# PSUM pool ends, operand tiles and load placement in a two-layer feed-forward block on one Trainium2 core

## The chip, the core and the metric

One core of one Trainium2 chip runs the whole program in one launch. The metric is device time in microseconds (us). Before the change the median of three runs is 2013.85 us (2013.82 to 2015.16). The core has five engines with queues of their own: PE (TensorE, matrix products), DVE (VectorE), ACT (ScalarE), POOL (GpSimd) and SP (which here only issues transfers). PE reads both operands from the on-chip memory SBUF and writes into PSUM, which has eight banks of 2 KiB per partition.

## The reference

One encoder layer on x of 512 rows and 2048 columns, all float32. The parts that matter here come last:

```
h = RMSNorm(x); z = h @ w_in; A = MLA(z); N = neighbourhood attention(z)
x = x + concat(RMSNorm(A), RMSNorm(N)) @ w_out
x = x + relu(RMSNorm(x) @ w_ff1)^2 @ w_ff2        # d_ff = 8192
y = RMSNorm_final(x)
```

## The kernel before, in words

Every float32 operand is kept as two tiles, a rounded high part ("hi") and the remainder ("lo"), and every block product is three matmuls: hi by hi, lo by hi, hi by lo (`mm3`, L100; `prod`, L287 and L968). `split` (L90) makes the two parts: a cast on ACT (L92 or L95), a subtraction on DVE (L93 or L96).

The program runs through attention until 540 us of the profile, the output projection "wo" until about 702 us, and then the two feed-forward products.

**From the projection to the first product.** The projection is made in four column blocks n. For each, the new x is written to DRAM (`x_d`), scaled (`hs`), transposed by PE into PSUM tiles `ht` (L811), and `mix` (L750) makes from the four `ht` tiles the operands of the first product: a11, a12, a22 and the sums s1 to s4 of a Strassen scheme, each as hi and lo and in two halves g. The `ht` tiles lie in pool `ps_ax` (`sct`, `trt`, `pvt`, four banks), projection results in pool `ps_mm` (`mmt`, four banks). After the last `mix` both pools are closed and a pool `ps_w` is opened over the same eight banks, with four tiles of two banks:

```
close_pool("ps_ax")
close_pool("ps_mm")
ps_w = open_pool("ps_w", space=PSUM)
def wide(name): return ps_w.tile([P, 2, 512], F32, name=name, tag="w", bufs=4)
```

**First product** (`ff1_pair`, L858, calling `strassen_t`, L285). 32 pairs of column blocks; each pair is seven products (a11, a12, s2, s1, s3, s4, a22, in this order) of 24 matmuls with 256 columns, accumulated into PX, PY and PZ, each in the first bank of a `wide` tile. The moving operand is an a or s tile, the weights of the array are the block of w_ff1 (tiles `ob`, `ot`). Nine of the operand pairs lie in pool `ops1`, one pool tile per operand part of 2*UNIT+16 elements (UNIT is 1024; 8,256 bytes), three more in slots of pool `iop` at an offset of 8 elements, two in other pools. A finished pair is squared by ACT and written to DRAM, the part a to `f_d`, sums of it to `s_d`.

**Second product.** It takes the 8192 rows of w_ff2 in nine chunks (`CH`, L31): a plain one of 512 (`plain`, L935: eight groups of 24 matmuls with 512 columns, tiles `f`), seven of 1024 made by a Strassen scheme (`spair`, L950: two pairs per chunk, each of seven products of 24 matmuls, tiles `sx`, `sy`, `sz`; I call one such call a Strassen pair), and a plain one of 512 at the end (tiles `f2l`). Here the reloaded first result is the weights (`fo`, loaded by `load_op`, L929, into the `ops1` tiles at an offset of 8 elements) and w_ff2 is the moving operand (tiles `hi` and `lo` of pool `wp`, and by `f2_bufs`, L906, every third time an `ops1` tile). Raw loads of 512 KB go through three buffers (`raw_unit`, L70). The seven `fo` operands of the first Strassen chunk are loaded ahead of the plain chunk. DVE adds every finished PSUM tile into the sum SF.

**Tail.** x is read back from `x_d` (`load_x1`, L1033) into four operand pairs (`xf`), SF and the last chunk are added, and the final norm is written out.

The order on each queue is set by a scheduler that follows program order and the readiness of buffers.

Of the kernel before, what the change touches and what calls it, by code (L numbers as in the profile page):

```python
# [36 lines left out]
def block_kernel(ctx, tc, x, xT, w_c, w_ckv, w_qkv, w_uqn, w_uqr, w_ukv, rpb, gcols, w_out, w_ff1, w_ff2, g_fin,  # L37
# [17 lines left out]
    ps_mm = open_pool("ps_mm", space=PSUM)  # L55
    ps_ax = open_pool("ps_ax", space=PSUM)

# [226 lines left out]

    def strassen_t(nm, getA, b, m1, tile, v, t2, pst=None):  # L285

# [10 lines left out]
        b11, b21, b12, b22 = b  # L297
        PX, PY, PZ = ((pst or mmt)(f"p{x}{nm}")[:, :256] for x in "xyz")
        prod(PX, "a11", opB(f"ob11{nm}", b11), True)
# [374 lines left out]

    def wide_tile(pool, name, tag, off, bufs=1, dt=F32R):
        return pool.tile([P, UNIT + 16], dt, name=name, tag=tag, bufs=bufs)[:, off:off + UNIT]

    def op_pair(nm, g, name, off):
        t = ops1.tile([P, 2 * UNIT + 16], F32R, name=name, tag=f"{nm}_{g}")
        return [t[:, off + j * UNIT:off + (j + 1) * UNIT] for j in range(2)]  # L680

    def iot(name, off=0):
        return [wide_tile(iop, f"{name}_{j}", f"io{j}", off, 4) for j in range(2)]

# [55 lines left out]
    def opt(pool, nm, g):  # L740
        if pool is iop:
            t = iot(f"{nm}_{g}", 8)
        elif pool is ops1:
            t = op_pair(nm, g, f"{nm}_{g}", 0)
        else:
            t = [pool.tile([P, UNIT], F32R, name=f"{nm}_{g}_{j}") for j in range(2)]
        A[nm][g] = [v.rearrange("p (k n) -> p k n", k=4) for v in t]
        return A[nm][g]
# [39 lines left out]
    for n in range(4):  # L788
# [4 lines left out]
        if n == 3:  # L793
            first = [wide_tile(iop, f"b{kh}1_0", f"io{kh}", 0, 4, F32) for kh in range(2)]
            for kh in range(2):
                nc.sync.dma_start(out=first[kh], in_=w_ff1[kh, 1])
# [61 lines left out]
    def ff1_pair(i):  # L858
# [3 lines left out]
        t2 = sb(rk, "t2", i, UNIT, 1) if i else wp.tile([P, UNIT], F32, name="t2_0", tag="raw", bufs=3)  # L862
        PX = strassen_t(f"_{i}", getA, b, sb(rk, "m1", i, 256, 1), lambda t, w: sb(rk, t, i, w, 1), v, t2,
                        lambda s: wide(s)[:, 0])
        nc.scalar.activation(v[0][:, 256:], PX, AF.Relu)
# [15 lines left out]
    close_pool("ps_ax")  # L881
    close_pool("ps_mm")
    ps_w = open_pool("ps_w", space=PSUM)

    def wide(name):
        return ps_w.tile([P, 2, 512], F32, name=name, tag="w", bufs=4)

    for i in range(DFF // 256):
        ff1_pair(i)
    close_pool("rk")  # L890
    close_pool("vp")


# [6 lines left out]

    def op_tiles(nm, g, name):
        return op_pair(nm, g, name, 8)

    nb = [0]

    def f2_bufs(name):  # L906
        i = nb[0] % 6
        nb[0] += 1
        return unit_bufs(name) if i < 4 else op_tiles(("a11", "s3")[i - 4], 1, name)

# [7 lines left out]
    def load_f(c, q):  # L918
        raw = raw_unit(f_d[c][:, :, q, :], f"fa{c}_{q}", 4)
        t = blocks(op_tiles(("a11", "a12")[q], 0, f"fa{c}_{q}") if c else iot(f"fa{c}_{q}"))  # L920
        split(t[0], t[1], raw)
        F.setdefault(c, []).append(t)
# [6 lines left out]
    def load_op(c, nm):  # L929
        raw = raw_unit((f_d if nm[0] == "a" else s_d)[c][:, BLK[nm]], f"fo{c}_{nm}", 4)  # L930
        t = blocks(op_tiles(nm, 0, f"fo{c}_{nm}"))
        split(t[0], t[1], raw)
        FO[c, nm] = t
# [16 lines left out]
    def spair(c, j, k0, hook):  # L950
# [4 lines left out]
        def ld(kh, nh, u):  # L955
            name = f"sb{kh}{nh}_{nm}_{u}"
            if nh == 0:
                t = wide_tile(iop, name, f"io{kh}", 0, 4, F32)
            else:
                t = fb.tile([P, UNIT], F32, name=name, tag=("b12", "b22")[kh], bufs=2)  # L960
            nc.sync.dma_start(out=t, in_=w_ff2[k0 // 256 + kh * nu + u, 2 * j + nh])
            return t
# [68 lines left out]
    RF = 36  # L1031

    def load_x1(m):  # L1033
        xs = []
        for h, t in enumerate(op_tiles(("s3", "s4", "a22", "a11")[m], m // 3, f"xf{m}")):
            t = t.bitcast(F32)
            xs += [t[:, :512], t[:, 512:]]
        for n in range(4):
# [4 lines left out]
    for n in range(4):  # L1043
        if n == 1:
            xfs = [load_x1(0)]
        for g in range(2):
# [19 lines left out]
    for m in range(NM):  # L1066
# [18 lines left out]
        for n in (0, 3, 1, 2):  # L1085
# [77 lines left out]
```

## Time and profile before

| | |
|---|---|
| Median of three runs | 2013.85 us |
| Profiled execution | 2013.5 us, span 2011.7 us |
| PE busy | 1968.0 us (98% of the span), 12540 instructions |
| DVE busy | 1573.3 us (78%) |
| ACT busy | 1005.1 us (50%) |
| Mean granted PE clock | 0.994 of full speed |

The span is what the engines' instructions cover; 1.8 us of the execution lie around it. PE is nearly always busy, but a matmul's length is not fixed: the interval from one start to the next is what counts. The clock column of a stretch is the granted share of the full clock (2.4 GHz); 0.5 is the lower level of 1.2 GHz.

### The profile page before, as it was taken

How to read it: one execution, taken by the hardware profiler on the slowest of the kernel's cores; microseconds unless marked ns; L12 is line 12 of the kernel's file. 1: busy time of each engine (PE TensorE's matmuls, PEld its weight loads, DVE VectorE, ACT ScalarE, POOL GpSimd, SP SyncE). 2: the span in 40 equal slices, each digit the busy share in tenths (PEclk: the TensorE clock that was granted, in tenths of full speed). 3: DMA queues.
4: the chain of work that ended last, by engine and by line, in shares of the span. 5: the costliest groups of instructions: out<-in, count | busy, mean ns of one | idle time of the engine just before them, and what ended most of it. 6: DMA issues, size and time to landing. Idle time of an engine off the chain costs nothing.

```text
span 2011.7 us, 31103 instructions
## 1 busy us (share of the span) xinstructions
PE 1968.0 (98%) x12540; PEld 1775.4 (88%) x12540; DVE 1573.3 (78%) x1892; ACT 1005.1 (50%) x1435; POOL 64.0 (3%) x73
## 2 busy tenths in 40 slices
PE   8999999999999979999999999998999999999997
PEld 7999999888887779999999999997888888888886
DVE  7777777787435767787878787875799999999995
ACT  5645445566314545555555555554454454444443
POOL 2000010100000000000000000000000000000000
PEclk9999999999999989999999999999999999999999
DMA  8354454431334333545454444455364354444342
GB/s 279 131 180 154 160 167 139 143 102 58 119 107 157 120 132 122 183 138 178 140 175 143 172 146 169 153 168 214 126 196 168 117 178 160 143 158 156 126 165 97
DMA packets 121552, 303.75 MB, mean 151 GB/s; under 512 B 10688, under 2 KB 49344, under 8 KB 121152
## 3 DMA queue, kind: packets, MB, share of 16 engines
q1 hardware_dynamic: 98416, 271.09, 40.7%
q10 hardware_dynamic: 22224, 29.52, 4.1%
q8 instruction: 98, 1.61, 0.3%
q0 software_dynamic: 768, 1.15, 0.2%
q14 instruction: 46, 0.38, 0.1%
HBM read 250.60 MB, written 52.26 MB: 151 GB/s over the span
## 4 chain that ended last, share of the span: by engine, by line
PE 91%; DVE 3%; DMA 3%; ACT 1%; issue 1%; POOL 1%; SPq 0%; POOLq 0%; DVEq 0%; ACTq 0%
PE px L292 7%; PE px L293 7%; PE px L294 7%; PE sx L980 5%; PE sx L979 5%; PE sx L981 5%; PE pz L293 4%; PE pz L292 4%; PE pz L294 4%; PE wo L102 3%; PE wo L103 3%; PE wo L104 3%; PE sz L979 3%; PE sz L981 3%; PE sz L980 3%; PE py L292 2%
## 5 line engine op out<-in xcount | busy, mean ns | idle before, releaser
L190 DVE TENSOR_TENSOR SF<-SF,sx 128x1024 f32<-128x1024 f32 x56 | 68.1, 1216 | 2.3 <-PE sx L981 1.1
L190 DVE TENSOR_TENSOR sb<-sb,sb 128x1024 f32<-128x1024 f32 x56 | 67.2, 1220 | 0.5
L92 ACT CAST s_0hi<-sb 128x1024 fp32r<-128x1024 f32 x28 | 29.5, 1052 | 41.5 <-PE sx L981 18.4
L128 POOL TENSOR_TENSOR stat<-stat,nhalf 128x1 f32<-128x1 f32 (+1 forms) x6 | 4.4, 730 | 1401.5 <-DVE stat L127 1401.5
L92 ACT CAST a<-sb 128x1024 fp32r<-128x1024 f32 x30 | 31.5, 1050 | 32.1 <-PE sz L981 15.3
L92 ACT CAST a_0hi<-sb 128x1024 fp32r<-128x1024 f32 x27 | 28.4, 1052 | 35.4 <-PE sz L981 17.1
L92 ACT CAST s<-sb 128x1024 fp32r<-128x1024 f32 x28 | 29.4, 1050 | 30.8 <-PE sx L981 16.5
L93 DVE TENSOR_TENSOR a_0lo<-sb,a_0hi 128x1024 fp32r<-128x1024 f32 x27 | 33.0, 1221 | 13.3 <-ACT a_0hi L92 13.3
L93 DVE TENSOR_TENSOR a<-sb,a 128x1024 fp32r<-128x1024 f32 x30 | 36.6, 1220 | 7.5 <-ACT a L92 7.5
L868 ACT ACTIVATE v<-v 128x512 f32<-128x512 f32 x64 | 40.5, 632 | 2.0
L867 ACT ACTIVATE v<-v 128x512 f32<-128x512 f32 x64 | 40.3, 630 | 1.4 <-DVE v L190 0.3
L92 ACT CAST a_1hi<-sb 128x1024 fp32r<-128x1024 f32 x27 | 28.3, 1047 | 23.8 <-PE sz L981 17.1
L92 ACT CAST s_1hi<-sb 128x1024 fp32r<-128x1024 f32 x28 | 29.4, 1049 | 19.2 <-PE sx L981 18.8
L190 DVE TENSOR_TENSOR b<-b,b 128x1024 f32<-128x1024 f32 x32 | 38.9, 1215 | 0.0
L93 DVE TENSOR_TENSOR s_0lo<-sb,s_0hi 128x1024 fp32r<-128x1024 f32 x28 | 34.2, 1221 | 4.5 <-ACT s_0hi L92 4.5
L93 DVE TENSOR_TENSOR s<-sb,s 128x1024 fp32r<-128x1024 f32 x28 | 33.8, 1220 | 2.6 <-ACT s L92 2.6
L190 DVE TENSOR_TENSOR SF<-SF,sz 128x1024 f32<-128x1024 f32 x28 | 34.1, 1216 | 1.8 <-PE sz L981 1.7
L190 DVE TENSOR_TENSOR sb<-st,sb 128x1024 f32<-128x1024 f32 x28 | 34.1, 1219 | 0.1
L190 DVE TENSOR_TENSOR st<-sb,sb 128x1024 f32<-128x1024 f32 x28 | 34.1, 1219 | 0.1
L93 DVE TENSOR_TENSOR s_1lo<-sb,s_1hi 128x1024 fp32r<-128x1024 f32 x28 | 34.1, 1218 | 0.0
L93 DVE TENSOR_TENSOR a_1lo<-sb,a_1hi 128x1024 fp32r<-128x1024 f32 x27 | 32.9, 1218 | 0.0
L93 DVE TENSOR_TENSOR wo_2lo<-wo_2r,wo_2hi 128x1024 fp32r<-128x1024 f32 x8 | 9.8, 1224 | 27.9 <-ACT wo_2hi L92 27.9
(2897 smaller groups left out, 8300.5 us busy)
## 6 DMA issues: line engine op xcount, KB each, us to landing
sb<-in_w_ff_dram SPq DMA_DIRECT2D x112, 512.0 KB, 4.5
b<-in_w_ff_dram SPq DMA_DIRECT2D x64, 512.0 KB, 5.9
f_d<-v ACTq DMA_DIRECT2D x32, 512.0 KB, 6.7
s_d<-sv SPq DMA_DIRECT2D x28, 512.0 KB, 6.4
nb<-in_w_qkv_dram SPq DMA_DIRECT2D x24, 512.0 KB, 4.5
xn<-in_x_dram SPq DMA_DIRECT2D x8, 512.0 KB, 4.9
X<-in_x_dram SPq DMA_DIRECT2D x16, 256.0 KB, 5.4
wo_0r<-in_w_out_dram SPq DMA_DIRECT2D x8, 512.0 KB, 4.4
```

The costliest lines, as they stand in the source:

```text
L92: i = nc.scalar.copy(hi, src)
L93: nc.vector.tensor_tensor(out=lo, in0=src, in1=hi.bitcast(F32), op=ALU.subtract)
L102: nc.tensor.matmul(ps, ah, bh, start=first, stop=False)
L103: nc.tensor.matmul(ps, ah, bl, start=False, stop=False)
L104: nc.tensor.matmul(ps, al, bh, start=False, stop=last)
L190: nc.vector.tensor_tensor(out=out, in0=a, in1=b, op=op)
L292: nc.tensor.matmul(ps, bh, ah, start=first and kk == 0, stop=False, **kw)
L293: nc.tensor.matmul(ps, bh, al, start=False, stop=False, **kw)
L294: nc.tensor.matmul(ps, bl, ah, start=False, stop=kk == 7, **kw)
L979: nc.tensor.matmul(ps[:, mm], ah, bh, start=first and kk == 0, stop=False, **kw)
L980: nc.tensor.matmul(ps[:, mm], ah, bl, start=False, stop=False, **kw)
L981: nc.tensor.matmul(ps[:, mm], al, bh, start=False, stop=kk == 2 * nu - 1, **kw)
```

## The change

**PSUM.** `ps_ax` opens at the other end of PSUM; `ps_mm` keeps the first four banks, `ps_ax` the last four. PX, PY and PZ of the first product are now `mmt` tiles of `ps_mm`, which stays open until the first product is over. The wide tiles of the second product come from two pools of two tiles, one over the banks of `ps_ax`, one over those of `ps_mm`.

**Operands.** The `ops1` tiles become two tiles, `op_a` of six operand pairs and 64 more elements, and `op_b` of three pairs and 48 more. Operand parts follow each other at 1024 elements; the first product uses them at offset 0, the second at offset 8. Slots of `iop` lose their 16 extra elements and their offset.

**Loads.** The seven `fo` loads of the first Strassen chunk are placed two after each block n of the plain chunk; the two loads of the last chunk's `fa` follow products a11 and a12 of the last Strassen pair. x is read back for three row blocks into a tile `xb` that takes the place of all of `op_b`, and for the fourth into a tile of its own.

```diff
-    ps_ax = open_pool("ps_ax", space=PSUM)
+    ps_ax = open_pool("ps_ax", space=PSUM, side="right")
...
-        PX, PY, PZ = ((pst or mmt)(f"p{x}{nm}")[:, :256] for x in "xyz")
+        PX, PY, PZ = (mmt(f"p{x}{nm}")[:, :256] for x in "xyz")
...
-    def wide_tile(pool, name, tag, off, bufs=1, dt=F32R):
-        return pool.tile([P, UNIT + 16], dt, name=name, tag=tag, bufs=bufs)[:, off:off + UNIT]
-
-    def op_pair(nm, g, name, off):
-        t = ops1.tile([P, 2 * UNIT + 16], F32R, name=name, tag=f"{nm}_{g}")
-        return [t[:, off + j * UNIT:off + (j + 1) * UNIT] for j in range(2)]
-
-    def iot(name, off=0):
-        return [wide_tile(iop, f"{name}_{j}", f"io{j}", off, 4) for j in range(2)]
+    def io_slot(name, j, dt=F32R):
+        return iop.tile([P, UNIT], dt, name=name, tag=f"io{j}", bufs=4)
+
+    def iot(name):
+        return [io_slot(f"{name}_{j}", j) for j in range(2)]
...
+    OPA = [(nm, 0) for nm in ("a11", "a12", "s2", "s1")] + [("a11", 1), ("s3", 1)]
+    OPB = [(nm, 0) for nm in ("s3", "s4", "a22")]
+    op_a = ops1.tile([P, 2 * len(OPA) * UNIT + 64], F32R, name="op_a", tag="op_a")
+    op_b = ops1.tile([P, 2 * len(OPB) * UNIT + 48], F32R, name="op_b", tag="op_b")
+
+    def op_pair(nm, g, off):
+        t, l = (op_a, OPA) if (nm, g) in OPA else (op_b, OPB)
+        i = l.index((nm, g))
+        return [t[:, off + (2 * i + j) * UNIT:off + (2 * i + j + 1) * UNIT] for j in range(2)]
+
...
     close_pool("ps_ax")
-    close_pool("ps_mm")
-    ps_w = open_pool("ps_w", space=PSUM)
-
-    def wide(name):
-        return ps_w.tile([P, 2, 512], F32, name=name, tag="w", bufs=4)
-
+    ps_w = [open_pool("ps_w0", space=PSUM, side="right")]
     for i in range(DFF // 256):
         ff1_pair(i)
     close_pool("rk")
     close_pool("vp")
+    close_pool("ps_mm")
+    ps_w.append(open_pool("ps_w1", space=PSUM))
+    nw = [0]
+
+    def wide(name):
+        i = nw[0] // 2 % 2
+        nw[0] += 1
+        return ps_w[i].tile([P, 2, 512], F32, name=name, tag="w", bufs=2)
...
-    for nm in ORDER:
-        load_op(1, nm)
     for n in range(4):
         plain(0, n, 0)
+        for nm in ORDER[2 * n:2 * n + 2]:
+            load_op(1, nm)
...
-            for q in range(2):
-                load_f(NC_ - 1, q)
-            spair(c, 1, k0, lambda a: None)
+            spair(c, 1, k0, lambda a: load_f(NC_ - 1, ("a11", "a12").index(a)) if a in ("a11", "a12") else None)
...
+    xb = ops1.tile([P, 2 * len(OPB) * UNIT + 48], F32, name="xb", tag="op_b")
+    x3 = lpool.tile([P, D], F32, name="x3")
```

PE's order where the first product begins, before: the last transposes (`ht`, from the scaled rows `hs`) and then the first product's matmuls (`px`, moving operand a, weights `ob`).

```order
L811 MATMUL ht_2_7220<-ident,hs_6510 128x128
L811 MATMUL ht_2_7220<-ident,hs_6511 128x128
L811 MATMUL ht_3_7225<-ident,hs_6509 128x128
L811 MATMUL ht_3_7225<-ident,hs_6510 128x128
L811 MATMUL ht_3_7225<-ident,hs_6511 128x128
L292 MATMUL px_7323<-a_0_6689,ob_0hi 128x256
L293 MATMUL px_7323<-a_0_6689,ob_0hi 128x256
L294 MATMUL px_7323<-a_0_6689,ob_0lo 128x256
```

The same place after the change, from the last matmul of the projection (`wo`) on:

```order
L104 MATMUL wo_3_3_7066<-wo_3_3hi,aT_1_6492 128x512
L292 MATMUL px_7315<-op_a,ob_0hi 128x256
L293 MATMUL px_7315<-op_a,ob_0hi 128x256
L817 MATMUL ht_0_7203<-ident,hs_6510 128x128
L817 MATMUL ht_1_7208<-ident,hs_6510 128x128
L817 MATMUL ht_2_7213<-ident,hs_6510 128x128
L817 MATMUL ht_3_7218<-ident,hs_6510 128x128
L294 MATMUL px_7315<-op_a,ob_0lo 128x256
```

The first product's matmuls have moved ahead of and in between the transposes.

DVE's order at the same place, before: `t` is the difference that the seventh product's weights `ot` are made from, `ob_0lo` and `ot_0lo` are remainders of weights, `a_1_1` the remainder of a22's second half, made from the `ht` tiles, and `v` the sums of finished products.

```order
L190 TENSOR_TENSOR t_0_7321<-b_0r,t_0_7321 128x1024
L93 TENSOR_TENSOR s_1_1_7267<-hr,s_1_0_7266 128x1024
L832 SCALAR_TENSOR_TENSOR stat<-stat 128x4
L833 RECIPROCAL stat<-stat 128x4
L96 SCALAR_TENSOR_TENSOR a_1_1_7279<-ht_0_7210,gc,a_1_0_7278 128x256
L96 SCALAR_TENSOR_TENSOR a_1_1_7279<-ht_1_7215,gc,a_1_0_7278 128x256
L96 SCALAR_TENSOR_TENSOR a_1_1_7279<-ht_2_7220,gc,a_1_0_7278 128x256
L96 SCALAR_TENSOR_TENSOR a_1_1_7279<-ht_3_7225,gc,a_1_0_7278 128x256
L93 TENSOR_TENSOR ot_0lo<-b_0_7198,ot_0hi 128x1024
L190 TENSOR_TENSOR v_7320<-py_7324,m_0_7322 128x256
L93 TENSOR_TENSOR ob_0lo<-b_0_7199,ob_0hi 128x1024
L93 TENSOR_TENSOR ot_0lo<-t_0_7321,ot_0hi 128x1024
```

After:

```order
L93 TENSOR_TENSOR ob_0lo<-b_0_7192,ob_0hi 128x1024
L96 SCALAR_TENSOR_TENSOR a_1_1_7272<-ht_0_7203,gc,a_1_0_7271 128x256
L96 SCALAR_TENSOR_TENSOR a_1_1_7272<-ht_1_7208,gc,a_1_0_7271 128x256
L96 SCALAR_TENSOR_TENSOR a_1_1_7272<-ht_2_7213,gc,a_1_0_7271 128x256
L96 SCALAR_TENSOR_TENSOR a_1_1_7272<-ht_3_7218,gc,a_1_0_7271 128x256
L839 RECIPROCAL stat<-stat 128x4
L190 TENSOR_TENSOR v_7312<-py_7316,m_0_7314 128x256
L190 TENSOR_TENSOR v_7312<-px_7315,z_0_7347 128x256
L190 TENSOR_TENSOR t_0_7313<-b_0r,t_0_7313 128x1024
L190 TENSOR_TENSOR v_7312<-pz_7317,u_0_7346 128x256
L93 TENSOR_TENSOR ot_0lo<-t_0_7313,ot_0hi 128x1024
```

The remainder of s4's weights (`ob_0lo`) now stands ahead of the four a22 remainders, and the difference `t` has moved behind the sum `v` that reads the finished product s3 from `px`.

SP's order of loads between the two products, before: `fa` and `fo` are operands of the plain and the first Strassen chunk from DRAM, `w_0_n_g` the plain chunk's weights, `sb` the Strassen chunk's.

```order
L74 DMA fa_1r<-f_d_7293 128x4x256
L74 DMA fo_a11r<-f_d_7294 128x1024
L74 DMA fo_a12r<-f_d_7294 128x1024
L74 DMA fo_s2r<-s_d_7303 128x1024
L961 DMA sb_1_0_0_15087<-in_w_ff_dram 128x1024
L74 DMA fo_s1r<-s_d_7303 128x1024
L74 DMA fo_s3r<-s_d_7303 128x1024
L74 DMA fo_s4r<-s_d_7303 128x1024
L961 DMA sb_1_0_1_15089<-in_w_ff_dram 128x1024
L74 DMA fo_a22r<-f_d_7294 128x1024
L77 DMA w_0_0_0r<-in_w_ff_dram 128x1024
L77 DMA w_0_0_1r<-in_w_ff_dram 128x1024
```

After:

```order
L74 DMA fa_1r<-f_d_7286 128x4x256
L77 DMA w_0_0_0r<-in_w_ff_dram 128x1024
L77 DMA w_0_0_1r<-in_w_ff_dram 128x1024
L966 DMA sb_1_0_0_15078<-in_w_ff_dram 128x1024
L74 DMA fo_a11r<-f_d_7287 128x1024
L966 DMA sb_1_0_0_15074<-in_w_ff_dram 128x1024
L966 DMA sb_1_0_1_15076<-in_w_ff_dram 128x1024
L74 DMA fo_a12r<-f_d_7287 128x1024
L77 DMA w_0_1_0r<-in_w_ff_dram 128x1024
L77 DMA w_0_1_1r<-in_w_ff_dram 128x1024
L966 DMA sb_1_0_1_15080<-in_w_ff_dram 128x1024
L74 DMA fo_s2r<-s_d_7296 128x1024
```

The two loads of the plain chunk's first block (`w_0_0_0r`, `w_0_0_1r`) now stand right behind the `fa` loads, where the `fo` loads of a11 and a12 stood.

## Rows read from the trace of the kernel before

**Rows 1.** Page, section 4: the chain that ended last, by engine

```profile
PE 91%; DVE 3%; DMA 3%; ACT 1%; issue 1%; POOL 1%; SPq 0%; POOLq 0%; DVEq 0%; ACTq 0%
```

**Rows 2.** Windows: busy us of PE, PEld, DVE, ACT, POOL; clock; DMA

```profile
705.80:719.00 13.20, 0.09 (x1) 0.12 (x1) 12.67 (x27) 7.32 (x16) 0.00 (x0) 0.65 0.67 238
1365.60:1380.00 14.40, 14.36 (x49) 11.09 (x50) 6.88 (x6) 6.59 (x7) 0.00 (x0) 0.78 0.88 316
1450.00:1900.00 450.00, 450.00 (x1949) 366.14 (x1948) 433.74 (x379) 210.27 (x205) 0.00 (x0) 1.00 0.48 156
```

**Rows 3.** Timeline before the first product: start, duration (us), engine, line, out<-in, idle

```profile
704.33 1.42 PE L811 MATMUL ht<-ident,hs 128*128 128x128 f32 x11 [0.19 <-ACT hs L108]
...
714.21 1.22 DVE L190 TENSOR_TENSOR t<-b_0r,t 128x1024 f32<-128x1024 f32 x1
...
718.91 0.55 PE L292 MATMUL px<-a,ob_0hi 128*128 128x256 f32 x1 [13.16 <-DVE a L96]
```

**Rows 4.** Timeline, PE: the first matmul of the second pair of blocks

```profile
740.98 0.28 PE L292 MATMUL px<-a,ob_1hi 128*128 128x256 f32 x1
```

**Rows 5.** Timeline, PE: where products of one pair begin, and the next

```profile
760.94 0.28 PE L292 MATMUL px<-a,ob_2hi 128*128 128x256 f32 x1
...
766.66 0.28 PE L292 MATMUL px<-s,ot_2hi 128*128 128x256 f32 x1
...
769.51 0.28 PE L292 MATMUL pz<-s,ot_2hi 128*128 128x256 f32 x1
...
775.20 0.28 PE L292 MATMUL pz<-s,ob_2hi 128*128 128x256 f32 x1
...
778.02 0.28 PE L292 MATMUL px<-a,ot_2hi 128*128 128x256 f32 x1
...
780.90 0.28 PE L292 MATMUL px<-a,ob_3hi 128*128 128x256 f32 x1
```

**Rows 6.** Timeline, ACT: the last copy out of a finished pair

```profile
781.94 0.38 ACT L865 ACTIVATE v<-px 128x256 f32<-128x256 f32 x1
```

**Rows 7.** Timeline, SP queue: first operand load, first plain weight load

```profile
1341.56 0.33 SPq L74 DMA_DIRECT2D fo_a11r<-f_d  x1
...
1359.95 0.33 SPq L77 DMA_DIRECT2D w_0r<-in_w_ff_dram  x1
```

**Rows 8.** Timeline between the products: cast, remainder, first matmul of the plain chunk

```profile
1364.41 1.05 ACT L92 CAST w_0hi<-w_0r 128x1024 fp32r<-128x1024 f32 x1
...
1365.48 1.23 DVE L93 TENSOR_TENSOR w_0lo<-w_0r,w_0hi 128x1024 fp32r<-128x1024 f32 x1 [0.34 <-ACT w_0hi L92]
...
1365.51 0.80 PE L102 MATMUL f<-w_0hi,fa 128*128 128x512 f32 x1 [5.23 <-ACT w_0hi L92]
```

**Rows 9.** Timeline, PE: third and fourth group of the plain chunk begin

```profile
1379.85 0.39 PE L102 MATMUL f<-w_0hi,fa 128*128 128x512 f32 x1
...
1385.31 0.39 PE L102 MATMUL f<-w_0hi,fa 128*128 128x512 f32 x1
```

**Rows 10.** Timeline, PE: where products of the first Strassen pair begin

```profile
1412.76 0.40 PE L979 MATMUL sx<-a_0hi,fo_a 128*128 128x512 f32 x1
...
1423.92 0.39 PE L979 MATMUL sx<-s_0hi,fo_s 128*128 128x512 f32 x1
...
1429.43 0.39 PE L979 MATMUL sz<-s_0hi,fo_s 128*128 128x512 f32 x1
...
1434.88 0.39 PE L979 MATMUL sx<-s,fo_s 128*128 128x512 f32 x1
...
1440.42 0.39 PE L979 MATMUL sz<-s_0hi,fo_s 128*128 128x512 f32 x1
...
1446.01 0.39 PE L979 MATMUL sx<-a_0hi,fo_a 128*128 128x512 f32 x1
...
1451.59 0.40 PE L979 MATMUL sx<-a,fo_a 128*128 128x512 f32 x1
```

**Rows 11.** Timeline, SP queue: reload of the residual for the tail

```profile
1950.87 8.76 SPq L1039 DMA_DIRECT2D xf<-x_d  x12
```

More of the change, by code (lines that the diff above doesn't have):

```diff
@@ L283, in at, with strassen_t @@
         tasks.sort(key=lambda t: t[:2])
-    def strassen_t(nm, getA, b, m1, tile, v, t2, pst=None):
+    def strassen_t(nm, getA, b, m1, tile, v, t2):
         def prod(ps, a, bop, first):
@@ L741, in opt @@
         if pool is iop:
-            t = iot(f"{nm}_{g}", 8)
+            t = iot(f"{nm}_{g}")
         elif pool is ops1:
-            t = op_pair(nm, g, f"{nm}_{g}", 0)
+            t = op_pair(nm, g, 0)
         else:
@@ L793, in block_kernel @@
         if n == 3:
-            first = [wide_tile(iop, f"b{kh}1_0", f"io{kh}", 0, 4, F32) for kh in range(2)]
+            first = [io_slot(f"b{kh}1_0", kh, F32) for kh in range(2)]
             for kh in range(2):
@@ L862, in ff1_pair @@
         t2 = sb(rk, "t2", i, UNIT, 1) if i else wp.tile([P, UNIT], F32, name="t2_0", tag="raw", bufs=3)
-        PX = strassen_t(f"_{i}", getA, b, sb(rk, "m1", i, 256, 1), lambda t, w: sb(rk, t, i, w, 1), v, t2,
-                        lambda s: wide(s)[:, 0])
+        PX = strassen_t(f"_{i}", getA, b, sb(rk, "m1", i, 256, 1), lambda t, w: sb(rk, t, i, w, 1), v, t2)
         nc.scalar.activation(v[0][:, 256:], PX, AF.Relu)
@@ L899, in sf @@
         return SF[m // 2][:, n, m % 2, :]
-    def op_tiles(nm, g, name):
-        return op_pair(nm, g, name, 8)
     nb = [0]
@@ L908, in f2_bufs @@
         nb[0] += 1
-        return unit_bufs(name) if i < 4 else op_tiles(("a11", "s3")[i - 4], 1, name)
+        return unit_bufs(name) if i < 4 else op_pair(("a11", "s3")[i - 4], 1, 8)
     def blocks(t):
@@ L919, in load_f @@
         raw = raw_unit(f_d[c][:, :, q, :], f"fa{c}_{q}", 4)
-        t = blocks(op_tiles(("a11", "a12")[q], 0, f"fa{c}_{q}") if c else iot(f"fa{c}_{q}"))
+        t = blocks(op_pair(("a11", "a12")[q], 0, 8) if c else iot(f"fa{c}_{q}"))
         split(t[0], t[1], raw)
@@ L930, in load_op @@
         raw = raw_unit((f_d if nm[0] == "a" else s_d)[c][:, BLK[nm]], f"fo{c}_{nm}", 4)
-        t = blocks(op_tiles(nm, 0, f"fo{c}_{nm}"))
+        t = blocks(op_pair(nm, 0, 8))
         split(t[0], t[1], raw)
@@ L957, in ld @@
             if nh == 0:
-                t = wide_tile(iop, name, f"io{kh}", 0, 4, F32)
+                t = io_slot(name, kh, F32)
             else:
@@ L1031, in block_kernel @@
     RF = 36
+    xb = ops1.tile([P, 2 * len(OPB) * UNIT + 48], F32, name="xb", tag="op_b")
+    x3 = lpool.tile([P, D], F32, name="x3")
     def load_x1(m):
[L1034 to L1037, printed above, removed]
+        t = xb[:, m * D:(m + 1) * D] if m < 3 else x3
+        xs = [t[:, n * 512:(n + 1) * 512] for n in range(4)]
         for n in range(4):
@@ L1054, in block_kernel @@
             else:
-                u = op_tiles(("s2", "s1")[g], 0, f"wl{n}_{g}")
+                u = op_pair(("s2", "s1")[g], 0, 8)
             split(u[0], u[1], raw)
@@ L1092, in block_kernel @@
             (nc.sync if n % 2 else nc.scalar).dma_start(out=out[m * P:(m + 1) * P, sl], in_=xs)
-    for name in ("lpool", "sfp", "ops1", "iop", "ps_w", "wp", "const"):
+    for name in ("lpool", "sfp", "ops1", "iop", "ps_w0", "ps_w1", "wp", "const"):
         close_pool(name)
```

## The prediction

> **What bounds the kernel now.** I read the chain of waits first: PE carries 91% of the path that ended last [rows 1]. So a microsecond counts only where PE stands idle, where its clock is halved, or where the interval between matmuls can shrink. I then read the timeline at the stage borders that the change touches. Before the first product PE finishes its transposes at 704.33 + 1.42 = 705.75 and starts again at 718.91, with the gap put down to the last a22 remainder on DVE [rows 3]. In that stretch DVE is busy for 12.67 of 13.20 us and the granted clock falls to 0.65 on the mean [rows 2]: the lower level shows up only after PE has stood. Between the products PE stands for 5.23 us for a weight cast [rows 8], and the 14.4 us after it run at 0.78 [rows 2]. Everywhere else in the two products PE has no gap (450.00 of 450.00 us in the Strassen stretch [rows 2]); there only the interval from start to start is left, so I compared products of equal shape [rows 5, 10].
>
> **Start of the first product.** In the kernel before, `px` takes banks that the transposes' tiles held, so it needs their last reader, the a22 remainder. After, `px` lies in banks whose last readers are the projection's additions, and PE's order puts a11 round the transposes. The transposes still end near 705.75, and a11's rest ends near 707.05 (11 matmuls of 0.12 us). Five products of 2.85 us [rows 5] then end near 721.3, with about 0.6 us lost where s2's remainder on DVE is late: 721.9. What is late next is the weights of the seventh product. DVE makes the difference `t` now behind a sum that reads s3's result, about 719.0, and behind the four a22 remainders, so near 721.1 to 722.3; with a cast of 1.05 and a remainder of 1.23 [rows 8] its first matmuls start near 723.5 and the third near 724.8. The product then ends near 727.6, against 740.98 before [rows 4]. Gain 13.4 us. Contained in it is the clock: the first pair took 740.98 - 718.91 = 22.07 us where a later one takes 780.90 - 760.94 = 19.96 [rows 4, 5], and waits of 1 to 3 us, I assume, do not bring the lower level back. Bounds: with no wait for the seventh product 16.2; with the wait and 2.1 us at the lower clock, and 2 us more on a full DVE, 9.
>
> **Interval in the first product.** Each pair runs the same seven products of 24 matmuls, yet a22 takes 780.90 - 778.02 = 2.88 us, s4 778.02 - 775.20 = 2.82, s2 2.85, a11 and a12 together 5.72, s1 and s3 together 5.69 [rows 5]. What differs is where the moving operand starts. The tiles before are 8,256 bytes, 32 times 256 and 64 over, so parts step by 64 bytes modulo 256. By the addresses that the built program holds, the weights stand at 64 and the moving halves (12 matmuls each) at 160/160 in a22, 96/96 in s4, 224/224 in s2, 160/32 in a11 and a12, 32/160 in s1, 224/96 in s3. That gives 120.0 ns a matmul for 160, 117.5 for 96, 118.75 for 224, and from a11 and a12 118.3 for 32; s1 and s3 then come to 5.69, as seen. After, ten of the fourteen halves stand at 32, one at 96 and the three in `iop` at 64, which is the weights' own place and occurs in no row with 256 columns. I take 117.5 for it, the lowest seen, since in the second product equal places are the fastest. A pair is then 12 x (10 x 118.3 + 117.5 + 3 x 117.5) ns = 19.84 us, 0.12 less, over 32 pairs 4.0 us. Bounds: 1.1 us (120.0 for the unseen place), 7.5 (4 ns below its neighbour, as in the second product).
>
> **Between the products.** The first plain weight load moves from 1359.95 to about where the first operand load was, 1341.56 [rows 7]. Its cast and remainder then lie before PE's last matmul of the first product, at 1360.3. The wait of 5.23 us goes, and with it the lower clock: two groups of the plain chunk took 1379.85 - 1365.51 = 14.34 us, where one at full clock takes 1385.31 - 1379.85 = 5.46 [rows 8, 9], so 3.4 us. Gain 8.6. The seven operand loads, now spread over the chunk's 47 us, compete with eight weight loads for three raw buffers; before, such fifteen loads were issued in about 37 us, so I cost this at nothing. If the second weight block comes late, 4 us of the gain are lost: bounds 4 to 9.
>
> **Interval in the second product.** Moving tiles stand at 64 modulo 256, the weights at 192 for a11, a12 and a22, 0 for s2 and s3, 128 for s4, and 64 for s1. One Strassen pair takes 1451.59 - 1412.76 = 38.83 us; s1, with both at the same place, takes 5.45 us, the others 5.51 to 5.59 [rows 10]. After, all stand at 64. At 5.48 us (s1 with its neighbours' rounding) a pair takes 38.36 us, 0.47 less, over 14 pairs 6.6 us; the last plain chunk's 192 matmuls, whose weights stood in the a11 and a12 tiles, give about 4 ns each, 0.8 us. Close behind PE is DVE, busy for 433.74 of 450 us [rows 2]; after, PE wants 444.6 us for that work, so DVE has 11 us of room there. Bounds: 0 (place is not the cause) to 8.
>
> The Trainium skill speaks against both interval terms: TensorE: Matmul & The Clock Gate, Back-to-back issue gap, gives the isolated gap as the columns over 2.4 GHz and about 2.5 ns, with no place of an operand in it, which would be about 109 ns for 256 columns and 216 for 512. The rows differ: 118 to 120 and 227 to 233, and unequal for equal columns. By that rule the sum would keep only the two border terms.
>
> **Tail.** x now comes back into all of `op_b`, so its twelve loads cannot start before the last a22 product ends, at 1956 rather than 1950.87; they took 8.76 us to issue [rows 11]. Four wide PSUM tiles give PE some 22 us before it needs the first addition. I cost it at 0, bounds a gain of 1 and a loss of 3. Smaller slots and the moved `fa` loads lie beside PE's work: 0.
>
> **Sum.** 13.4 + 4.0 + 8.6 + 6.6 + 0.8 = 33.4 us off the profiled execution of 2013.5 (its span of 2011.7 and 1.8 around it) gives 1980.1; the median is 0.35 above that execution: 1980.4 us.
>
> **Rivals.** First, *the place does not set the interval*: then products differ by something that the new tiles do not change. For it: places and products go together one to one, so the rows cannot separate them. Against it: a11, a12 and a22 are alike in all else, yet a22 differs. Result: only 13.4 + 8.6 = 22.0 go, 1991.9 us.
>
> Second, *DVE becomes the bound*, at the start (12.67 of 13.20 us busy) and in the Strassen chunks, where a later copy or sum waits in line. The first term falls to 9, the second product's gain to 3: 9 + 4.0 + 8.6 + 3 + 0.8 = 25.4, 1988.5 us. For it are DVE's shares, against it that every Strassen chunk leaves it room.
>
> Third, *the change does not free the start*: a11 waits for something in the operand tile that is as late as the a22 remainder was. Then 20.0 are left, 1993.9. PE's order speaks against it.
>
> Fourth, and *slower than before*: PX, PY and PZ turn over in four one-bank tiles, and each next pair's `py` needs the finished pair's `px`, which ACT copies out last. The copy ends at 781.94 + 0.38 = 782.32 [rows 6], 1.42 us after the pair's end at 780.90, and `py` comes 2.86 us after it, so 1.44 us are spare. If in the new banks the copy is later than that, every pair pays: with more than 33.4/31 = 1.1 us per pair, a copy 2.5 us later than now, the sum turns; at 3 us later it costs 48 us, 2028. Against it: the tiles before were four as well, with the same turn.
>
> **How the numbers follow.** Forecast 0.62 (its own range 1973 to 1987), no effect of place 0.15, DVE 0.13, start not freed 0.04, slower 0.04, and 0.02 for gains and losses that cancel. Within 0.2% (4 us, about what a measurement can tell from no change) is 2009.8 to 2017.9. The first four cases are all faster: 0.94 less a little for what I have not seen, 0.92; same 0.03, slower 0.05. Range: 1973 (each term near its better bound) to 1993 (intervals unchanged, start a little worse).
>
> **What would show it.** Right: the first `px` before 706, the second pair's first matmul near 727.6, a pair of 19.84 us with equal a11, a12 and s3, no PE wait between the products, Strassen products all near 5.48. Wrong: products as unequal as now, a lower clock near the start, waits of `py` for ACT, or PE waits for a sum in the Strassen chunks or the tail.

## The result and the profile after

The changed kernel takes 1977.39 us (median of four runs, 1976.71 to 1979.67), the kernel before 2014.46 in the same comparison: ratio 0.9818, 95% interval 0.9801 to 0.9835. The profiled execution's span is 1974.9 us after 2011.7, 36.8 less. PE's starts in the two traces say where it went:

| us from the span's start | before | after | gained so far | in this stretch | forecast |
|---|---|---|---|---|---|
| projection's last matmul ends | 702.57 | 700.13 | 2.44 | 2.44 | 0 |
| second pair of the first product begins | 740.98 | 724.72 | 16.26 | 13.83 | 13.4 |
| first product ends | 1360.27 | 1342.66 | 17.61 | 1.34 | 4.0 |
| first Strassen matmul | 1412.76 | 1386.04 | 26.72 | 9.12 | 8.6 |
| last chunk's first matmul | 1956.28 | 1919.16 | 37.12 | 10.40 | 6.6 |
| end of the span | 2011.69 | 1974.93 | 36.76 | -0.36 | 0.8 |

The timeline of the changed kernel at the first product (start, duration, engine, line, out<-in, idle before):

```profile
699.97 0.28 PE L292 MATMUL px<-op_a,ob_0hi 128*128 128x256 f32 x1
...
720.76 0.39 PE L292 MATMUL px<-op_b,ot_0hi 128*128 128x256 f32 x1 [1.15 <-ACT ot_0hi L92]
...
722.02 0.38 PE L294 MATMUL px<-op_b,ot_0lo 128*128 128x256 f32 x1 [0.75 <-DVE ot_0lo L93]
...
724.72 0.28 PE L292 MATMUL px<-op_a,ob_1hi 128*128 128x256 f32 x1
```

The 13.16 us of [rows 3] are gone. In their place stand the two short waits of the seventh product, for the cast and the remainder of `ot`, as its difference is made late.

Windows of the changed kernel (us; busy us of PE, PEld, DVE, ACT, POOL with instructions; granted clock; DMA share; GB/s): the projection, the first product's start, the first product and the Strassen stretch.

```profile
540.00:695.00 155.00, 153.81 (x699) 126.75 (x699) 78.11 (x100) 60.16 (x92) 3.13 (x5) 1.00 0.41 143
700.00:724.70 24.70, 22.76 (x185) 21.89 (x184) 22.68 (x41) 17.31 (x31) 0.00 (x0) 1.00 0.52 188
740.00:1290.00 550.00, 550.00 (x4646) 550.00 (x4645) 434.58 (x498) 301.27 (x416) 0.00 (x0) 1.00 0.47 157
1450.00:1900.00 450.00, 450.00 (x1987) 372.63 (x1986) 438.83 (x385) 213.60 (x207) 0.00 (x0) 1.00 0.44 148
```

The same view of the kernel before, for the two stretches that [rows 2] did not hold:

```profile
540.00:695.00 155.00, 153.77 (x690) 125.15 (x690) 76.39 (x99) 60.13 (x92) 3.12 (x5) 1.00 0.42 143
740.00:1290.00 550.00, 550.00 (x4631) 550.00 (x4630) 429.83 (x490) 300.67 (x415) 0.00 (x0) 1.00 0.47 158
```

Where PE is busy throughout, the stretch divided by its matmuls is the mean interval. In the Strassen stretch it falls from 450/1949 = 230.9 ns [rows 2] to 450/1987 = 226.5; in the first product only from 118.8 to 118.4; and the projection, on which nothing was forecast, does nine matmuls more in equal time. At the first product's start the clock is 1.00 in this execution in spite of the short waits, against 0.65 in [rows 2]; below, under the longer `iop` slots, are executions in which it fell.

One pair of the first product in the changed kernel (timeline, PE; first matmuls of some halves, and of the next pair), to be set beside [rows 5]:

```profile
744.60 0.28 PE L292 MATMUL px<-op_a,ob_2hi 128*128 128x256 f32 x1
...
750.30 0.28 PE L292 MATMUL px<-op_a,ot_2hi 128*128 128x256 f32 x1
...
751.72 0.28 PE L292 MATMUL px<-s,ot_2hi 128*128 128x256 f32 x1
...
753.16 0.28 PE L292 MATMUL pz<-op_a,ot_2hi 128*128 128x256 f32 x1
...
764.50 0.28 PE L292 MATMUL px<-op_a,ob_3hi 128*128 128x256 f32 x1
```

The half of s2 in `op_a` takes 1.42 us, the half in `iop` (tile s, at the weights' own place) 1.44: 118.2 and 119.7 ns over all such halves of the trace. A pair takes 19.90 us, not 19.84.

The border between the products (timeline of the changed kernel), which answers to [rows 7, 8]:

```profile
1324.06 0.33 SPq L77 DMA_DIRECT2D w_0r<-in_w_ff_dram  x1
...
1334.09 1.05 ACT L92 CAST w_0hi<-w_0r 128x1024 fp32r<-128x1024 f32 x1 [1.53 <-PE pz L293]
...
1342.50 0.39 PE L102 MATMUL f<-w_0hi,fa 128*128 128x512 f32 x1
```

The load is issued 18 us and cast 8 us before use, and PE's row has no idle time.

Strassen products s1 and s3 of the changed kernel, and the next pair (timeline, PE), which answer to [rows 10]:

```profile
1386.04 0.39 PE L984 MATMUL sx<-a_0hi,op_a 128*128 128x512 f32 x1
...
1402.36 0.39 PE L984 MATMUL sz<-s_0hi,op_a 128*128 128x512 f32 x1
...
1407.80 0.39 PE L984 MATMUL sx<-op_a,op_b 128*128 128x512 f32 x1
...
1413.24 0.39 PE L984 MATMUL sz<-s_0hi,op_b 128*128 128x512 f32 x1
...
1424.12 0.39 PE L984 MATMUL sx<-op_a 128*128 128x512 f32 x1
```

s1 and s3 now take 5.44 us each, as all seven do: 38.08 a pair instead of 38.83. In the tail the reload comes late (SP queue and first addition, timeline of the changed kernel):

```profile
1919.35 5.78 SPq L1043 DMA_DIRECT2D xb<-x_d  x12
...
1923.28 0.75 DVE L1082 SCALAR_TENSOR_TENSOR xb<-f2l,stat,xb 128x512 f32<-128x512 f32 x1
...
1924.09 0.50 PE L102 MATMUL f2l<-wl,op_a 128*128 128x512 f32 x1 [0.35 <-DVE xb L1082]
```

The last chunk's own interval fell (its matmuls at one place took 232 ns and take 227.5), but two waits of 0.7 us together for `xb` and other lags give that back.

### The profile page after: what moved, and what is told of

It reads as the page before. It is cut to its first block, busy times and chain, and to the rows that moved or that the text cites. A ratio compares the mean times of both kernels' runs of the same rounds, so it can differ in the third digit from the quotient of the medians.

```text
span 1974.9 us, 31118 instructions
## 1 busy us (share of the span) xinstructions
PE 1947.9 (99%) x12540; PEld 1769.1 (90%) x12540; DVE 1569.1 (79%) x1892; ACT 1005.2 (51%) x1435; POOL 65.2 (3%) x73
## 3 DMA queue, kind: packets, MB, share of 16 engines
q0 software_dynamic: 768, 1.15, 0.2%
## 4 chain that ended last, share of the span: by engine, by line
PE 86%; DVE 6%; DMA 4%; issue 2%; ACT 1%; POOL 1%; SPq 0%; POOLq 0%; DVEq 0%; ACTq 0%
PE px L292 7%; PE px L293 7%; PE px L294 7%; PE sx L986 5%; PE sx L985 5%; PE sx L984 5%; PE pz L293 4%; PE pz L292 4%; PE pz L294 4%; PE wo L102 3%; PE wo L104 3%; PE wo L103 3%; PE sz L986 2%; PE sz L985 2%; PE sz L984 2%; PE py L294 2%
## 5 line engine op out<-in xcount | busy, mean ns | idle before, releaser
L92 ACT CAST op_a<-sb 128x1024 fp32r<-128x1024 f32 x58 | 61.1, 1053 | 62.0 <-PE sx L986 25.5
L93 DVE TENSOR_TENSOR op_a<-sb,op_a 128x1024 fp32r<-128x1024 f32 x58 | 70.3, 1217 | 6.9 <-ACT op_a L92 6.9
L92 ACT CAST a_0hi<-sb 128x1024 fp32r<-128x1024 f32 x27 | 28.4, 1054 | 35.1 <-PE sz L986 16.6
L984 PE MATMUL sx<-op_a,op_b 128*128 128x512 f32 x80 | 31.1, 389 | 0.0
L985 PE MATMUL sx<-op_a,op_b 128*128 128x512 f32 x80 | 31.1, 389 | 0.0
```

The lines of the kernel that those rows point to most:

```text
L92: i = nc.scalar.copy(hi, src)
L93: nc.vector.tensor_tensor(out=lo, in0=src, in1=hi.bitcast(F32), op=ALU.subtract)
L984: nc.tensor.matmul(ps[:, mm], ah, bh, start=first and kk == 0, stop=False, **kw)
L985: nc.tensor.matmul(ps[:, mm], ah, bl, start=False, stop=False, **kw)
```

## The experiments

All are the changed kernel with one edit, unless said otherwise. Times are medians; "before" was measured beside each group at 2012.98, 2014.16, 2014.41 and 2013.81 us. Where a few us matter I read the stage from the trace, since the projection's first matmul comes between 497.6 and 501.4 us in the kept executions. Eight medians lie above the range that was expected: 0.5 us for the tiles undone and for the longer slots, 2.7 for offset 24 in the second product, 3.1 and 10.2 for offset 16 and 24 in the first, 1.8 for offset 16 with the shifted pool, 2.5 for offset 0 and 21.3 for all halves at 128.

**The PSUM part undone.**

```diff
-    ps_w = [open_pool("ps_w0", space=PSUM, side="right")]
+    close_pool("ps_mm")
+    ps_w = open_pool("ps_w", space=PSUM)
...
-        PX, PY, PZ = (mmt(f"p{x}{nm}")[:, :256] for x in "xyz")
+        PX, PY, PZ = ((pst or mmt)(f"p{x}{nm}")[:, :256] for x in "xyz")
```

> The changed kernel with its PSUM pools as before: px, py and pz again wait for the transposes' banks. Theory (the start was freed by the banks): PE stands about 13 us before the first product again, the clock falls to its lower level there, the second pair begins some 14 us later, and the time is 1990 to 1993 us; intervals of both products stay as in the changed kernel. Rival (the start was freed by the operand tiles or by the shorter projection): no such gap, 1976 to 1980 us.

Measured 1991.82 us. The timeline, and the window of the gap:

```profile
717.39 0.55 PE L292 MATMUL px<-op_a,ob_0hi 128*128 128x256 f32 x1 [13.16 <-DVE a L96]
```

```profile
704.30:717.40 13.10, 0.01 (x1) 0.04 (x1) 12.65 (x27) 7.31 (x16) 0.00 (x0) 0.67 0.67 240
```

The gap is 13.16 us again, with the same releaser and a clock of 0.67 against 0.65; the second pair begins 14.0 us later, the projection's own shift taken off. Both products keep the changed kernel's intervals. So the banks are the cause of this term, and of no other.

**The load order undone.**

```diff
+    for nm in ORDER:
+        load_op(1, nm)
     for n in range(4):
         plain(0, n, 0)
-        for nm in ORDER[2 * n:2 * n + 2]:
-            load_op(1, nm)
```

> The changed kernel with the seven fo loads ahead of the plain chunk again. Theory (the load order made the wait between the products): PE stands about 5 us before the plain chunk, the clock falls and the chunk's first two groups take some 3.4 us more; 1985 to 1987 us. Rival (the wait went for another reason, such as an earlier end of the DMA traffic): the gap stays below 1 us, 1976 to 1980 us.

Measured 1986.56 us. The first matmul of the plain chunk:

```profile
1347.74 0.80 PE L102 MATMUL f<-w_0hi,fa 128*128 128x512 f32 x1 [5.88 <-ACT w_0hi L92]
```

From the first product's end to the first Strassen matmul PE needs 9.0 us more than in the changed kernel: the wait, and 2.9 us in the chunk.

**The operand tiles undone**: the kernel before with the PSUM and load parts.

```diff
-    ps_ax = open_pool("ps_ax", space=PSUM)
+    ps_ax = open_pool("ps_ax", space=PSUM, side="right")
...
-    for nm in ORDER:
-        load_op(1, nm)
     for n in range(4):
         plain(0, n, 0)
+        for nm in ORDER[2 * n:2 * n + 2]:
+            load_op(1, nm)
```

> The kernel before with only the PSUM part and the load part of the change, operand tiles and slots as before. Theory (the operands' places set the intervals): a pair of the first product takes 19.96 us again, a Strassen pair 38.8, the projection is some 2.5 us longer than in the changed kernel; 1990 to 1993 us, with the start and the border between the products as short as in the changed kernel. Rival (the intervals became shorter because of the other PSUM banks): intervals as in the changed kernel, 1976 to 1980 us.

Measured 1993.46 us. Its windows of the projection and the Strassen stretch:

```profile
540.00:695.00 155.00, 153.77 (x690) 125.20 (x691) 75.98 (x98) 60.47 (x92) 3.13 (x5) 1.00 0.42 143
1450.00:1900.00 450.00, 450.00 (x1949) 365.97 (x1948) 432.56 (x378) 208.06 (x202) 0.00 (x0) 1.00 0.45 150
```

690 and 1949 matmuls, as in the kernel before, while start and border stay short. The tiles set the intervals, the projection's too.

**Another offset in the second product** (24 instead of 8, in the four places that set it, of which one is shown).

```diff
-        t = blocks(op_pair(nm, 0, 8))
+        t = blocks(op_pair(nm, 0, 24))
```

> The changed kernel with offset 24 instead of 8 in the second product, so that the weights' tiles and every third moving tile stand 64 bytes further on, modulo 256. Theory (the distance between moving and weights modulo 256 sets the interval): two of three Strassen blocks now have a distance of 192, which had 233 ns before the change, and one of three stays at 0 with 227: 2352 x 2/3 x 6.3 ns = 9.9 us more in the Strassen pairs and about 1 us in the last chunk; 1987 to 1989 us. Rival (the two padded tiles as such are what helps, wherever they start): unchanged, 1976 to 1980 us.

Measured 1991.74 us. The Strassen stretch:

```profile
1450.00:1900.00 450.00, 450.00 (x1947) 364.15 (x1946) 432.09 (x377) 207.35 (x201) 0.00 (x0) 1.00 0.45 148
```

1947 matmuls, against the kernel before's 1949, from an edit of one constant. In the trace 1560 matmuls with moving tile and weights unequal take 233.3 ns and 791 with both at the same place 227.5. The Strassen pairs are 11.1 us longer (9.9 expected). That two padded tiles as such would help is refuted.

**Longer `iop` slots** (16 elements more, offset 8 for its operands).

```diff
-        return iop.tile([P, UNIT], dt, name=name, tag=f"io{j}", bufs=4)
+        return iop.tile([P, UNIT + 16], dt, name=name, tag=f"io{j}", bufs=4)[:, off:off + UNIT]
```

> The changed kernel with the slots of pool iop 16 elements longer again and offset 8 for the three operands there, as before the change; op_a and op_b stay. Theory (these slots also hold the projection's weights side, so their length set its interval): the projection takes 2.6 us more than in the changed kernel, three quarters of its matmuls at 229 to 233 ns; the first product, whose three iop operands leave the weights' own place, 0.9 us less; 1978 to 1981 us. Rival (the projection is shorter because of the PSUM banks or by chance): its time is as in the changed kernel.

Measured 1981.49 us. The projection's window:

```profile
540.00:695.00 155.00, 153.77 (x690) 125.18 (x690) 76.30 (x99) 60.26 (x92) 3.12 (x5) 1.00 0.42 143
```

The projection is 2.6 us longer again: its weights (`nT`, `aT`) lie in these slots. The pairs of the first product went from 19.90 to 19.86 us, 1.2 us over 30 pairs, where 0.9 was expected; a longer wait for the copy of `u` in the thirty-first pair (1.7 us instead of 0.64) takes most of it back. Another 0.9 us is lost in the tail, which stays open, and 1.5 at the first product's start. This last is no effect of the edit. The kept executions of five experiments have it: this one, offset 16 with and without the shifted pool, the residual's block, and offset 0 in the second product, and the last two change nothing at the start. The seventh product's waits are there as in the changed kernel (1.1 to 1.3 us and 0.8), but behind them the clock falls. From the run with the residual's block:

```profile
722.00:726.00 4.00, 4.00 (x23) 4.00 (x23) 3.97 (x4) 1.45 (x2) 0.00 (x0) 0.57 0.39 132
```

In these five the second pair begins 26.0 to 26.1 us after the projection's end, in the seven other kept executions without the 13 us gap, the changed kernel's among them, 24.5 to 24.6. What decides between the two was not tested.

**Offset 16, 24 and 40 in the first product** (the edit of 16 is shown).

```diff
-            t = op_pair(nm, g, 0)
+            t = op_pair(nm, g, 16)
```

> The changed kernel with offset 16 instead of 0 for op_a and op_b in the first product, so that nine of its fourteen operand halves stand at 96 modulo 256 instead of 32. Theory (only the distance between the moving operand and the weights matters): these 3456 matmuls go from 118.2 to 116.9 ns, 4.5 us less: 1972 to 1974 us. Rival (116.9 belongs to the one operand s4 and its other pool): unchanged, 1976 to 1980 us.

> The changed kernel with offset 24 instead of 0 for op_a and op_b in the first product: nine of fourteen operand halves stand 64 bytes beyond the weights, modulo 256, a distance that 383 matmuls of s4 showed at 113.4 ns in the kernel with the shifted pool. Theory: 3456 matmuls go from 118.2 to 113.4 ns, 16.6 us less, 1959 to 1963 us, and the first product's pair takes 19.38 us. Rival (113.4 ns belongs to s4's own pool, or DVE and ACT cannot follow a pair of 19.4 us): 1968 to 1978 us, with PE waits inside the pairs.

> The same with offset 40: a distance of 128, which no run has shown at 256 columns. Theory of place: another interval for the same 3456 matmuls and no other stage moved; between 113.4 and 119.9 ns, 16.6 us less to 5.9 us more than the changed kernel: 1960 to 1983 us. Rival (a larger offset as such is faster): 113.4 ns or less, 1961 us or less.

Measured 1977.05, 1973.18 (1972.47 to 1975.01; ratio to the kernel before 0.9798, interval 0.9782 to 0.9815) and 1980.11 us. The first product's window, of offset 16:

```profile
740.00:1290.00 550.00, 550.00 (x4662) 550.00 (x4661) 434.81 (x499) 302.00 (x416) 0.00 (x0) 1.00 0.47 158
```

of offset 24:

```profile
740.00:1290.00 550.00, 550.00 (x4690) 550.00 (x4689) 434.62 (x500) 304.27 (x420) 0.00 (x0) 1.00 0.48 160
```

and of offset 40:

```profile
740.00:1290.00 550.00, 550.00 (x4646) 550.00 (x4645) 434.14 (x498) 301.93 (x416) 0.00 (x0) 1.00 0.47 157
```

Means of 118.0, 117.3 and 118.4 ns. Offset 40 stayed within its bounds and refutes that a larger offset as such is faster. 16 and 24 gained 1.8 and 5.1 us in the stage where 4.5 and 16.6 were expected, and both times lie in the ranges of their rivals. The rivals' reasons do not hold all the same: halves in `op_a` reach the interval of s4's own pool, and PE has no wait inside the pairs but one of about 1 us in the thirty-first. Halves of one pair with offset 24 (timeline, PE) show more:

```profile
764.89 0.28 PE L292 MATMUL px<-op_a,ob_3hi 128*128 128x256 f32 x1
767.61 0.28 PE L292 MATMUL py<-op_a,ob_3hi 128*128 128x256 f32 x1
768.97 0.28 PE L292 MATMUL py<-a,ob_3hi 128*128 128x256 f32 x1
770.41 0.28 PE L292 MATMUL px<-op_a,ot_3hi 128*128 128x256 f32 x1
771.83 0.29 PE L292 MATMUL px<-s,ot_3hi 128*128 128x256 f32 x1
...
778.96 0.28 PE L292 MATMUL pz<-op_b,ob_3hi 128*128 128x256 f32 x1
...
780.38 0.28 PE L292 MATMUL pz<-s,ob_3hi 128*128 128x256 f32 x1
```

a11 and the first half of a12 take 113.3 ns a matmul (2.72 and 1.36 us). Then comes a12's half in `iop`, 1.44 us, and after it the halves at the fast place take 1.42, the first half of s4 too (the last two lines), whose weights are an `ob` as those of a11 are. In the next pair a11 starts at 113.3 again. So an interval is not set by a half's own place alone; what ran before counts.

**Offset 16, and pool `iop` 32 bytes further on.**

```diff
+    iop.tile([P, 8], F32, name="iopad")
...
-            t = op_pair(nm, g, 0)
+            t = op_pair(nm, g, 16)
```

> As the kernel with offset 16 in the first product, and all of pool iop 32 bytes further on, so that its three operands stand at 96 too instead of the weights' own place. Theory: 1152 matmuls more go from 119.7 to 116.9 ns, 3.2 us less; the projection's and the plain chunk's weights then stand 32 bytes behind the moving operand, a distance that no run has shown at 512 columns: between 0 and 6 us more. 1969 to 1977 us. Rival (what made these three operands slow is something else than their place): the first product as with offset 16 alone.

Measured 1978.78 us. Windows of the projection and the first product:

```profile
540.00:695.00 155.00, 153.79 (x687) 124.06 (x686) 74.35 (x97) 60.18 (x92) 3.13 (x5) 1.00 0.43 144
740.00:1290.00 550.00, 550.00 (x4719) 550.00 (x4719) 436.47 (x503) 305.75 (x422) 0.00 (x0) 1.00 0.48 162
```

With no half left at the weights' place, the halves at 96 take 116.7 ns on the mean, against 117.6 with offset 16 alone, and s4's second half, which the pads moved to 128, 113.4. The pairs gained 8.7 us; the projection (233.2 ns) and the plain chunk gave 5.4 back, and the first product's start 1.5 more, with the lower clock told above. Place was the cause for the three slow operands.

**The residual's first block in the tile of its own.**

```diff
-        t = xb[:, m * D:(m + 1) * D] if m < 3 else x3
+        t = xb[:, (m - 1) * D:m * D] if m else x3
```

> The changed kernel with the residual's first row block in the tile of its own and the other three in xb. Theory (the first additions of the tail are late because xb is free only after the last Strassen product): the first addition into a finished tile comes 1 us or more earlier and PE's two waits of 0.7 us for xb go; the last chunk takes 0.5 us less, the total 0 to 1 us less. Rival (DVE's own queue, not the load, sets the additions): nothing moves.

Measured 1977.84 us. The last chunk's first wait (timeline):

```profile
1924.06 0.47 PE L102 MATMUL f2l<-wl_0hi,op_a 128*128 128x512 f32 x1 [0.89 <-DVE SF L190]
```

The waits for `xb` went and one of 0.89 us for SF came: the last chunk is 0.13 us shorter. DVE's queue sets the tail's start, and the late reload costs next to nothing.

**Offset 0 in the second product.**

```diff
-        t = blocks(op_pair(nm, 0, 8))
+        t = blocks(op_pair(nm, 0, 0))
```

> The changed kernel with offset 0 instead of 8 in the second product: two of three moving blocks there stand 32 bytes beyond the weights, a distance that no run has shown at 512 columns, the third block at the same place. Theory of place: 1560 matmuls of the Strassen pairs get an interval of their own between 226.7 and 233.3 ns, 0 to 10.3 us more; 1977 to 1989 us. Rival (only equal against unequal places matters at 512 columns): near 233 ns and the upper end.

Measured 1991.45 us. The Strassen stretch:

```profile
1450.00:1900.00 450.00, 450.00 (x1944) 364.34 (x1943) 431.58 (x376) 207.19 (x202) 0.00 (x0) 1.00 0.45 147
```

1560 matmuls 32 bytes apart take 233.4 ns: the rival's upper end. At 512 columns equal places are the fastest, 64 bytes is next (229), the other distances that a run has shown take 232 to 233.4.

**All halves of the first product at 128.**

```diff
+    iop.tile([P, 16], F32, name="iopad")
...
-            t = op_pair(nm, g, 0)
+            t = op_pair(nm, g, 24)
...
-            rk.tile([P, 8], F32, name="rkpad")
...
+    vp.tile([P, 40], F32, name="vpad")
```

> The changed kernel with all fourteen operand halves of the first product 64 bytes beyond the weights, modulo 256: offset 24 in op_a and op_b, pool iop 64 bytes further on, s4's and a22's second halves moved by pads. Theory (a half at this distance takes 113.4 ns, unless a half at the weights' own place runs between, as with offset 24 alone): a pair takes 19.05 us instead of 19.90, 27 us less over 32 pairs; the projection and the plain chunks, whose iop weights now stand 64 bytes ahead of the moving operand, go to 233 ns, 6 us more; 1954 to 1959 us. Rival (with offset 24 the products a11 and a12 alone are fast because of their weights ob, not because of what runs between): s1 to s4 and a22 stay at 118 ns, a pair takes 19.6 us, 1971 to 1976 us.

Measured: two of six runs at 1956.85 and 1961.42 us, four between 1978.93 and 1984.37; median 1980.27, ratio 0.9815, interval 0.9778 to 0.9852. The profiled execution is that of 1961.42. Its first product:

```profile
740.00:1290.00 550.00, 550.00 (x4856) 550.00 (x4855) 449.40 (x518) 317.92 (x434) 0.00 (x0) 1.00 0.49 166
```

550/4856 = 113.3 ns, all seven products alike; a pair takes 19.04 us, as expected, and the stage 22.2 us less. That settles s1 to s4 against the rival, up to the thirty-first pair of this execution. There PE waits for ACT, and what comes after is slower (timeline, PE; tiles `ob_30` are the thirty-first pair's, `ob_31` the last one's):

```profile
1281.57 0.28 PE L292 MATMUL px<-op_a,ob_30hi 128*128 128x256 f32 x1
...
1284.29 0.28 PE L292 MATMUL py<-op_a,ob_30hi 128*128 128x256 f32 x1
...
1295.06 0.38 PE L292 MATMUL px<-op_b,ot_30hi 128*128 128x256 f32 x1 [2.44 <-ACT u L307]
...
1305.17 0.28 PE L292 MATMUL px<-op_a,ob_31hi 128*128 128x256 f32 x1
...
1308.00 0.28 PE L292 MATMUL py<-op_a,ob_31hi 128*128 128x256 f32 x1
```

```profile
1295.00:1300.00 5.00, 4.94 (x29) 4.94 (x30) 3.98 (x6) 1.95 (x4) 0.00 (x0) 0.66 0.34 105
1300.00:1324.00 24.00, 24.00 (x206) 24.00 (x205) 16.83 (x17) 13.44 (x19) 0.00 (x0) 1.00 0.56 184
```

a11 takes 2.72 us before the wait and 2.83 after it, at the full clock again; every half of the last pair takes 117.8 ns, at places that have not moved. So the same program has two intervals. The four longer executions are some 22 us longer, and 4.5 ns for each of the 5376 matmuls would be 24 us, an estimate. That they ran at the slower interval is not shown, as no trace of them was kept. What selects the interval stays open.

## Why the prediction was right, step by step

**Start of the first product** (13.4, measured 13.83). Right in mechanism and in what came next: the waits for the seventh product's cast and remainder stand where the working put them. Undoing the PSUM part gave 14.0. The assumption that waits of 1 to 3 us do not bring the lower clock back holds for the kept execution, where the clock stayed at 1.00, but not for every one: in five experiments it fell behind the same waits and the gain was 1.5 us smaller.

**Between the products** (8.6, measured 9.12; undone, 9.0). Right, clock and second weight block included.

**Interval in the second product** (6.6, measured 10.40). The mechanism is right, since one constant gives all of it back. The size was off, and 10.40 lies beyond the step's better bound of 8. The mis-sized term is 5.48: the rows gave 5.45 us for s1, where all 24 matmuls stood at the weights' place, and I rounded that up. With all at one place a product takes 5.44 us, so a pair is 0.75 us shorter and not 0.47. That the moving tiles stand at 64 was not wholly right either: by the addresses of the built program one in six stood at 128.

**Interval in the first product** (4.0, measured 1.34). The mis-sized term is the unseen place. I took 117.5 ns for it because equal places are the fastest at 512 columns; at 256 they are among the slowest, 119.7. With that value the step's own formula gives 19.92 us a pair and 1.4 us over 32 pairs, near its lower bound of 1.1. A new wait of 0.64 us for the copy of `u` in the thirty-first pair lies in the measured 1.34 as well. The step also took a half's interval as a matter of its place alone, which offset 24 and the halves all at 128 contradict.

**Smaller slots, costed at 0** (measured 2.44 to the projection's end). The step "Smaller slots and the moved `fa` loads lie beside PE's work" failed. The `iop` slots also hold `nT` and `aT`, the projection's weights, whose four places became one: 231 ns on the mean before, 227.3 after. I had followed the slots only through the feed-forward part.

**Last chunk and tail** (0.8 forecast as a gain for the chunk's interval and nothing for the tail, 0.36 lost together). The interval fell as said, and the tail's loss is within its bounds.

The sum came near, 33.4 against 36.8, because 2.7 us too much in one term met 6.2 too little in two others, which is luck; the two border terms, 22.0 forecast and 22.95 measured, are not.

**Rivals.** That places do not set the interval was refuted by the two offsets in the second product. DVE did not become the bound: it is busy for 438.83 of 450 us in the Strassen stretch and PE still has no gap there. The start was freed. ACT's copy out of a pair did not hold `py`. The Trainium skill's rule (TensorE: Matmul & The Clock Gate, Back-to-back issue gap) has columns alone in it; no trace here agrees, as equal columns gave 113.3 to 120.0 ns at 256 and 226.7 to 233.4 at 512.

## What to carry to other kernels

Where PE is busy all the time, divide a stretch by its matmuls for each product of equal shape: unequal intervals point at where the operands stand, and an offset or pad of a few bytes is then worth trying, in several executions, for every stage that uses the same slots. A value measured at one column count does not carry over to another: measure the place itself. Before a pool is reopened over banks that a late reader holds, see whether the next stage can use banks that have long been free.

## What the runs showed of the hardware

Mean intervals of fp32r matmuls with 128 x 128 weights at the full clock over the kept executions, by the distance from weights to moving operand modulo 256 bytes. At 512 columns: 0, 226.7 to 228.7, and about 230 in some runs of only 12 or 24 such matmuls between others; 64, 229 to 231; 128 and 192, 232 to 233.3; -32 and 32, 233.2 and 233.4. At 256 columns: 0, 118.7 to 120.1; 32, 116.5 to 117.9; 64, 113.3 to 118.2 from half to half; 96, 119.7 to 119.9; 128, 118.6; 160, 117.6 to 118.6; 224, 118.1 to 118.3. At 256 columns, which are all of the first product, the weights stood at 64 in every run, so there the moving operand's own place and its distance from the weights are not separated. The best version found sets offset 24 in the first product alone: 1973.18 us, all of its runs below the changed kernel's, 5.1 us less in the first product from the second pair on.

The interval has a memory: at 256 columns and a distance of 64, matmuls ran at 113.3 ns until a half at distance 0 came between, and at 118 after it. With all halves at 64 they went from 113.3 to 117.8 behind a wait of 2.44 us, within one execution, and the program showed two groups of times 22 us apart from execution to execution. No run separated which operand or event decides it.

The clock fell to its lower level in or behind waits of 13.16 us (0.65 on the mean of the stretch), 5.23 us (0.78) and 2.44 us (0.66), and behind the pair of waits of 1.15 and 0.75 us in some executions (0.57) and not in others (1.00).
